# Moving the activation transposes of a fused matmul and rotary embedding from TensorE to VectorE

## The chip, the cores and the metric

The kernel runs on one core of a Trainium2 chip. The metric is the device time of one execution in microseconds (us). The kernel before takes 167.79 us (median of three runs, 167.52 to 168.66). Engine names in the profile lines are PE (TensorE matmul), PEld (TensorE weight load), DVE (VectorE), ACT (ScalarE), POOL (GpSimd) and SP (SyncE). ACTq and SPq are the queues from which ScalarE and SyncE issue their work, DMA transfers included. The span is the time from the first to the last instruction of the profiled execution, and the granted clock is the share of full TensorE speed that the chip's throttle allowed.

## The reference, cut to what matters

```python
batch, seq, hidden, n_heads = (16, 512, 768, 12)      # all arrays float32
y = np.matmul(x, weight)                              # (16*512, 768) @ (768, 768)
y = y.reshape(batch, seq, n_heads, head_dim)          # head_dim 64
y1, y2 = y[..., :32], y[..., 32:]
out1 = y1 * cos1 - y2 * sin1                          # cos, sin: (512, 64)
out2 = y2 * cos2 + y1 * sin2
out = np.concatenate([out1, out2], axis=-1)
```

The 8192 rows of x make 64 tiles of 128 rows, four tiles to a batch. The kernel's matmuls take x with the input columns on partitions, so each tile has to be transposed.

## The kernel before

A tile goes through these stages: SyncE loads it (393 KB), ScalarE casts it to fp16, TensorE transposes it in six 128x128 blocks by a matmul with the identity, ScalarE copies the result out of PSUM (the memory that matmuls write to), TensorE does 12 matmuls, VectorE does three multiplications (tv, and qv in two halves), GpSimd adds tv and qv, and ScalarE issues the store. The multiplications of a tile are called its rope below.

```python
    def stage_load(i):
        xs = xpool.tile([P, H], FP32, tag="xs")
        nc.sync.dma_start(out=xs, in_=xf[ts(i, P), :])          # 128 rows of 3072 B
    ...
    def stage_tp(i, eng):
        xc = x16[i]
        pt = pt_pool.tile([P, NKT, P], mm_dt, tag="pst")
        for kt in range(NKT):
            nc.tensor.transpose(pt[:, kt, :], xc[:, ts(kt, P)], ident)
        xT = tpool.tile([P, NKT, P], mm_dt, tag="xT")
        _copy(eng, xT, pt[:, :, :])
    ...
    for i in range(NMB):
        if i + 4 < NMB:
            stage_load(i + 4)
        if i + 2 < NMB:
            stage_cast(i + 2, nc.scalar)
        if i + 1 < NMB:
            stage_tp(i + 1, nc.scalar)
        stage_mm_rope(i)
        if i >= 3:
            stage_out(i - 3)            # nc.scalar.dma_start(...)
```

## Time and profile before

| | before |
|---|---|
| median time | 167.79 us |
| span of the profiled execution | 166.9 us |
| PE busy | 149.5 us (90%) |
| DVE busy | 125.4 us (75%) |
| one tile, start to start | 2.285 us |
| first tv starts at | 18.85 us |

These lines are from the page of the kernel before: the busy times of part 1, the chain of work that ended last (followed back from the last instruction, by engine), and five groups of instructions. A group's columns are line, engine, operation, tiles, shapes and count, then busy us and the mean ns of one, then the idle us just before them with what ended most of it.

```profile
PE 149.5 (90%) x1152; PEld 98.2 (59%) x1152; DVE 125.4 (75%) x202; ACT 97.2 (58%) x126; POOL 116.4 (70%) x68
...
PE 87%; DMA 4%; DVE 2%; ACT 1%; POOLq 1%; SPq 1%; issue 1%; DVEq 0%
...
L98 PE MATMUL psy<-w_sb,xT 128*128 128x512 f16 (+1 forms) x768 | 136.2, 328 | 0.0
...
L111 DVE TENSOR_TENSOR tv<-psy,cos_sb 128x768 f32<-128x768 f32 x64 | 61.2, 957 | 25.0 <-PE psy L98 23.2
L69 ACT COPY xT<-pt 128x768 f16<-128x768 f16 x63 | 50.2, 798 | 50.0 <-PE pt L87 41.7
L69 ACT CAST xc<-xs 128x768 f16<-128x768 f32 x62 | 51.7, 835 | 8.8 <-DMA xs<-in_x_dram 5.7
L87 PE MATMUL pt<-ident,xc 128*128 128x128 f16 x384 | 32.9, 224 | 10.2 <-DMA ident<-identity 9.1
```

TensorE is the engine that everything waits for: the chain is 87% PE, and VectorE's idle time is ended by psy, a matmul's result. The timeline of the kernel before shows one period. Its columns are start us, duration us, engine, line and operation, with idle time and releaser in brackets.

```profile
59.31 0.50 PE L87 MATMUL pt<-ident,xc 128*128 128x128 f16 x6
...
59.59 0.96 DVE L111 TENSOR_TENSOR tv<-psy,cos_sb 128x768 f32<-128x768 f32 x1 [0.40 <-PE psy L98]
...
59.65 2.11 PE L98 MATMUL psy<-w_sb,xT 128*128 128x512 f16 x12
...
61.60 0.50 PE L87 MATMUL pt<-ident,xc 128*128 128x128 f16 x6
...
61.87 0.96 DVE L111 TENSOR_TENSOR tv<-psy,cos_sb 128x768 f32<-128x768 f32 x1 [0.40 <-PE psy L98]
```

The six transposes start every 2.29 us, and the 12 matmuls start 0.34 us after them. VectorE is idle 0.40 us in each period.

### The profile page before, as it was taken

What the parts mean: (1) busy time and instruction counts of PE and PEld (TensorE: products, weight loads), DVE (VectorE), ACT (ScalarE), POOL (GpSimd) and SP (SyncE); (2) the same over time, 40 slices, a digit from 0 to 9 for tenths busy, and PEclk for the clock granted to TensorE, in tenths of its full rate; (3) what the DMA queues carried; (4) which work ended last, traced back from release to release, by engine and by line L of the source; (5) the groups of instructions that cost most, each with busy time, mean ns of one, the idle gap of its engine ahead of it and who ended that gap; (6) DMA issues with size and microseconds to landing.
All of it is one profiled execution on the core that took longest, in us unless ns stands there. A gap on an engine that the chain in (4) does not pass through costs nothing.

```text
span 166.9 us, 3238 instructions
## 1 busy us (share of the span) xinstructions
PE 149.5 (90%) x1152; PEld 98.2 (59%) x1152; DVE 125.4 (75%) x202; ACT 97.2 (58%) x126; POOL 116.4 (70%) x68
## 2 busy tenths in 40 slices
PE   0079799999999999999999999999999999999920
PEld 0065466666666666666666666666666666666610
DVE  1145499888898888888888888888888888888870
ACT  3150468666776666776666776666766667766100
POOL 0000099977778777787877788777787777887782
PEclk9999999999999999999999999999999999999997
DMA  5999789999999999999999999999999999834634
GB/s 190 300 394 404 290 286 262 381 379 368 335 356 376 321 343 351 339 350 337 348 342 351 373 331 339 361 325 348 350 329 376 320 352 320 341 152 164 244 151 170
DMA packets 20513, 53.20 MB, mean 319 GB/s; under 512 B 3345, under 2 KB 3345, under 8 KB 20497
## 3 DMA queue, kind: packets, MB, share of 16 engines
q1 hardware_dynamic: 11280, 27.82, 51.8%
q10 hardware_dynamic: 9216, 25.17, 37.7%
q8 instruction: 9, 0.15, 0.4%
q14 instruction: 8, 0.06, 0.1%
HBM read 27.82 MB, written 25.17 MB: 317 GB/s over the span
## 4 chain that ended last, share of the span: by engine, by line
PE 87%; DMA 4%; DVE 2%; ACT 1%; POOLq 1%; SPq 1%; issue 1%; DVEq 0%
PE psy L98 74%; PE pt L87 13%; DMA ident<-identity 4%; DVE tv L111 1%; POOLq L190 1%; ACT xc L69 1%; SPq L75 1%; DVE qv L116 1%; ACT xT L69 0%; DVEq L190 0%; DVE qv L113 0%; DVEq L111 0%
## 5 line engine op out<-in xcount | busy, mean ns | idle before, releaser
L120 POOL TENSOR_TENSOR ov<-tv,qv 128x768 f32<-128x768 f32 x64 | 116.2, 1817 | 47.0 <-DVE qv L116 45.0
L98 PE MATMUL psy<-w_sb,xT 128*128 128x512 f16 (+1 forms) x768 | 136.2, 328 | 0.0
L98 PEld LDWEIGHTS <-xT 128*128 128x128 f16 x768 | 73.1, 99 | 42.7 <-issue 1.3
L111 DVE TENSOR_TENSOR tv<-psy,cos_sb 128x768 f32<-128x768 f32 x64 | 61.2, 957 | 25.0 <-PE psy L98 23.2
L69 ACT COPY xT<-pt 128x768 f16<-128x768 f16 x63 | 50.2, 798 | 50.0 <-PE pt L87 41.7
L69 ACT CAST xc<-xs 128x768 f16<-128x768 f32 x62 | 51.7, 835 | 8.8 <-DMA xs<-in_x_dram 5.7
L87 PE MATMUL pt<-ident,xc 128*128 128x128 f16 x384 | 32.9, 224 | 10.2 <-DMA ident<-identity 9.1
L87 PEld LDWEIGHTS <-xc 128*128 128x128 f16 x384 | 27.6, 101 | 18.4 <-issue 5.1
L113 DVE TENSOR_TENSOR qv<-psy,tee_sb 128x384 f32<-128x384 f32 x64 | 35.0, 547 | 0.0
L116 DVE TENSOR_TENSOR qv<-psy,tee_sb 128x384 f32<-128x384 f32 x64 | 35.0, 547 | 0.0
L143 DVE CAST w_sb<-w_raw 128x768 f16<-128x768 f32 x6 | 3.4, 560 | 2.5 <-DMA w_raw<-in_weight_dram 2.5
L71 DVE CAST xc<-xs 128x768 f16<-128x768 f32 x2 | 1.1, 560 | 4.3 <-DMA xs<-in_x_dram 4.3
L71 DVE COPY xT<-pt 128x768 f16<-128x768 f16 x1 | 0.6, 558 | 4.5 <-PE pt L87 4.5
L69 ACT ACT_TABLE_LOAD x1 | 1.3, 1283 | 0.7 <-PEq L176 0.7
L176 POOL MEMSET const-float32-0.0<- 128x1 f32 x1 | 0.1, 98 | 0.2 <-issue 0.2
L144 DVE TENSOR_SCALAR tee_sb<-tee_sb 128x128 f32<-128x128 f32 x1 | 0.2, 218 | 0.0
L176 POOL MEMSET const-bfloat16-1.0<- 128x1 bf16 x1 | 0.1, 101 | 0.0
L176 POOL MEMSET const-uint8-127<- 128x1 uint8 x1 | 0.1, 101 | 0.0
L176 POOL MEMSET const-float32-1.0<- 128x1 f32 x1 | 0.1, 98 | 0.0
## 6 DMA issues: line engine op xcount, KB each, us to landing
xs<-in_x_dram SPq DMA_DIRECT2D x64, 384.0 KB, 5.3
out_dram<-ov ACTq DMA_DIRECT2D x64, 384.0 KB, 4.8
w_raw<-in_weight_dram SPq DMA_DIRECT2D x6, 384.0 KB, 6.8
cos_sb<-in_cos_dram SPq DMA_DIRECT2D x1, 128.0 KB, 6.4
tee_sb<-in_sin_dram SPq DMA_DIRECT2D x1, 128.0 KB, 6.4
ident<-identity SPq DMA_DIRECT2D x1, 32.0 KB, 6.4
```

Of the source, the lines that this page charges most:

```text
L69: eng.copy(out=o, in_=i_)
L71: eng.tensor_copy(out=o, in_=i_)
L75: nc.sync.dma_start(out=xs, in_=xf[ts(i, P), :])
L87: nc.tensor.transpose(pt[:, kt, :], xc[:, ts(kt, P)], ident)
L98: nc.tensor.matmul(psy[:, ds(noff, nsz)], xT[:, kt, :], w_sb[:, kt, ds(noff, nsz)], start=(kt == 0), stop=(kt == NKT - 1),)
L111: nc.vector.tensor_tensor(out=tv, in0=yh, in1=cbc, op=mybir.AluOpType.mult)
L113: nc.vector.tensor_tensor(out=qv[:, :, 0:HD], in0=yh[:, :, HD:D], in1=t1, op=mybir.AluOpType.mult)
L116: nc.vector.tensor_tensor(out=qv[:, :, HD:D], in0=yh[:, :, 0:HD], in1=t2, op=mybir.AluOpType.mult)
L120: nc.gpsimd.tensor_tensor(out=ov, in0=tv, in1=qv, op=mybir.AluOpType.add)
L143: nc.vector.tensor_copy(out=w_sb[:, kt], in_=w_raw[:, kt])
L176: nc = _bacc.Bacc("TRN2", target_bir_lowering=False, num_devices=1)
L190: with _tile.TileContext(nc) as tc:
```

## The change: intent and diff

The intent is to take all transposes off TensorE. The kernel uses the VectorE transpose as one within blocks of 32x32 elements, and leaves the rest of the transposition to the load: the 768 input columns of a batch are split into four quarters of 192, and quarter q is loaded onto partitions 32q to 32q+31. Two adjacent fp16 values are moved as one 4-byte element, so one instruction of 128x384 elements transposes a tile. The weights are loaded in a matching order. The work is now issued by batches of four tiles.

```diff
     def load(b, j0=0, nj=NJ):
...
+        for q in range(NQ):                       # four quarters, 32 partitions each
+            nc.sync.dma_start(
+                out=xss[b][ts(q, R), j0 : j0 + nj, :],
+                in_=x[b, ds(j0 * R, nj * R), ts(q, KQ)].rearrange("(j r) k -> r j k", r=R),
+            )
...
     def prepare(b, g0=0, ng=SB, eng=None):
...
+                nc.scalar.copy(out=x16[b][:, g], in_=src)
-            nc.tensor.transpose(pt[:, kt, :], xc[:, ts(kt, P)], ident)
+        nc.vector.transpose(
+            out=xTT[b][:, ds(g0, ng)].bitcast(FP32).rearrange("p g t j r -> p (g t j r)"),
+            in_=x16[b][:, ds(g0, ng)].bitcast(FP32).rearrange("p g t j r -> p (g t j r)"),
+        )
...
+    for i in range(NT, NMB - 1):
+        b, g = divmod(i, SB)
+        if g == 2 and 0 < b < B - 2:
+            load(b + 2)
+        ready = i + 1 if i == NT else i + 2
+        for n in range(ready, i + 3):
+            if n < NMB:
+                prepare(*divmod(n, SB), 1)        # cast and transpose of tile i + 2
+        for t in range(NT):
+            mm(i, t)
+        rope_whole(i)                             # tv and qv on VectorE, add on GpSimd
+        store(i - 3)                              # nc.scalar.dma_start(...)
```

The lines of this diff are picked from two whole kernels, with comments added, and cuts are marked with "...". The change also merges the two halves of qv into one VectorE instruction, moves the loads of the weights and of the cosine and sine tables to ScalarE's queue, sets other buffer counts, and computes the last tile in two halves.

More of the change, by code (lines that the diff above doesn't have):

```diff
@@ L7 @@
 import concourse.tile as tile
-from concourse import bass_utils, mybir
+from concourse import mybir
 from concourse.bass import ds, ts
@@ L13 @@
 FP16 = mybir.dt.float16
+MULT = mybir.AluOpType.mult
+ADD = mybir.AluOpType.add
 @with_exitstack
@@ L23 @@
     sin: bass.AP,
-    n_heads: bass.AP,
+    n_heads: int,
     out: bass.AP,
@@ L33 @@
     HD = D // 2
-    M = B * S
-    assert H % P == 0
-    NKT = H // P
-    NMB = M // P
+    R = 32
+    NQ = P // R
+    KQ = H // NQ
+    NT = KQ // (2 * R)
+    NMB = B * S // P
     SB = S // P
-    mm_dt = FP16
-    NSPLIT = [(0, 512), (512, H - 512)] if H > 512 else [(0, H)]
-    xf = x.rearrange("b s h -> (b s) h")
+    NSPLIT = [(0, 512), (512, H - 512)]
+    HALVES = [(0, H // 2), (H // 2, H // 2)]
     of = out.rearrange("b s h -> (b s) h")
     konst = ctx.enter_context(tc.tile_pool(name="konst", bufs=1))
-    ident = konst.tile([P, P], mm_dt)
@@ L50 @@
     cos_sb = konst.tile([P, SB, D], FP32)
     tee_sb = konst.tile([P, SB, D], FP32)
-    w_raw = konst.tile([P, NKT, H], FP32)
-    w_sb = konst.tile([P, NKT, H], mm_dt)
-    xpool = ctx.enter_context(tc.tile_pool(name="xpool", bufs=6))
-    cpool = ctx.enter_context(tc.tile_pool(name="cpool", bufs=3))
-    tpool = ctx.enter_context(tc.tile_pool(name="tpool", bufs=3))
-    opool = ctx.enter_context(tc.tile_pool(name="opool", bufs=4))
-    pt_pool = ctx.enter_context(tc.tile_pool(name="pt", bufs=2, space=bass.MemoryType.PSUM))
@@ L60 @@
-    py_pool = ctx.enter_context(tc.tile_pool(name="py", bufs=3, space=bass.MemoryType.PSUM))
-    xss = [None] * (NMB + 8)
-    x16 = [None] * (NMB + 8)
-    xTT = [None] * (NMB + 8)
-    ovs = [None] * NMB
-    def _copy(eng, o, i_):
-        if eng is nc.scalar:
-            eng.copy(out=o, in_=i_)
-        else:
-            eng.tensor_copy(out=o, in_=i_)
-    def stage_load(i):
-        xs = xpool.tile([P, H], FP32, tag="xs")
-        nc.sync.dma_start(out=xs, in_=xf[ts(i, P), :])
-        xss[i] = xs
@@ L78, in stage_cast @@
-    def stage_cast(i, eng):
-        xc = cpool.tile([P, H], mm_dt, tag="xc")
-        _copy(eng, xc, xss[i])
-        x16[i] = xc
-    def stage_tp(i, eng):
-        xc = x16[i]
-        pt = pt_pool.tile([P, NKT, P], mm_dt, tag="pst")
-        for kt in range(NKT):
-            nc.tensor.transpose(pt[:, kt, :], xc[:, ts(kt, P)], ident)
-        xT = tpool.tile([P, NKT, P], mm_dt, tag="xT")
-        _copy(eng, xT, pt[:, :, :])
-        xTT[i] = xT
-    def stage_mm_rope(i):
-        sb = i % SB
-        xT = xTT[i]
-        psy = py_pool.tile([P, H], FP32, tag="psy")
-        for kt in range(NKT):
-            for noff, nsz in NSPLIT:
-                nc.tensor.matmul(
-                    psy[:, ds(noff, nsz)],
-                    xT[:, kt, :],
-                    w_sb[:, kt, ds(noff, nsz)],
-                    start=(kt == 0),
-                    stop=(kt == NKT - 1),
-                )
-        yh = psy.rearrange("p (h d) -> p h d", d=D)
-        cbc = cos_sb[:, sb, :].unsqueeze(1).broadcast_to((P, NH, D))
-        t1 = tee_sb[:, sb, 0:HD].unsqueeze(1).broadcast_to((P, NH, HD))
-        t2 = tee_sb[:, sb, HD:D].unsqueeze(1).broadcast_to((P, NH, HD))
-        tv = tpool.tile([P, NH, D], FP32, tag="tv")
-        nc.vector.tensor_tensor(out=tv, in0=yh, in1=cbc, op=mybir.AluOpType.mult)
-        qv = tpool.tile([P, NH, D], FP32, tag="qv")
@@ new lines @@
+    w_raw = konst.tile([P, NT, 2, H], FP32)
+    w_sb = konst.tile([P, NT, 2, H], FP16)
+    xpool = ctx.enter_context(tc.tile_pool(name="xpool", bufs=3))
+    cpool = ctx.enter_context(tc.tile_pool(name="cpool", bufs=2))
+    tpool = ctx.enter_context(tc.tile_pool(name="tpool", bufs=2))
+    rpool = ctx.enter_context(tc.tile_pool(name="rpool", bufs=4))
+    opool = ctx.enter_context(tc.tile_pool(name="opool", bufs=5))
+    py_pool = ctx.enter_context(tc.tile_pool(name="py", bufs=4, space=bass.MemoryType.PSUM))
@@ new lines, with load, load_w @@
+    NJ = S // R
+    xss, x16, xTT, psys, ovs = {}, {}, {}, {}, {}
+    def load(b, j0=0, nj=NJ):
+        if b not in xss:
+            xss[b] = xpool.tile([P, NJ, KQ], FP32, tag="xs", name="xs")
+        for q in range(NQ):
[3 more added lines that the diff above has]
+            )
+    def load_w(t):
+        for q in range(NQ):
+            nc.scalar.dma_start(
+                out=w_raw[ts(q, R), t],
+                in_=weight[ds(q * KQ + t * 2 * R, 2 * R), :].rearrange(
+                    "(r e) n -> r e n", e=2
+                ),
+            )
@@ new lines, in prepare @@
+    def prepare(b, g0=0, ng=SB, eng=None):
+        if b not in x16:
+            x16[b] = cpool.tile([P, SB, NT, NQ, 2 * R], FP16, tag="xc", name="xc")
+            xTT[b] = tpool.tile([P, SB, NT, NQ, 2 * R], FP16, tag="xT", name="xT")
+        for g in range(g0, g0 + ng):
+            src = xss[b][:, ts(g, NQ), :].rearrange("p j (t r) -> p t j r", t=NT)
+            if eng is nc.vector:
+                nc.vector.tensor_copy(out=x16[b][:, g], in_=src)
+            else:
+                nc.scalar.copy(out=x16[b][:, g], in_=src)
+        nc.vector.transpose(
+            out=xTT[b][:, ds(g0, ng)].bitcast(FP32).rearrange("p g t j r -> p (g t j r)"),
+            in_=x16[b][:, ds(g0, ng)].bitcast(FP32).rearrange("p g t j r -> p (g t j r)"),
+        )
@@ new lines, in mm @@
+    def mm(i, t, parts=NSPLIT):
+        b, g = divmod(i, SB)
+        if i not in psys:
+            psys[i] = py_pool.tile([P, 2, 512], FP32, tag="psy", name="psy").rearrange(
+                "p b n -> p (b n)"
+            )
+        xT = xTT[b].rearrange("p g t j (r e) -> p g t j r e", e=2)
+        for e in range(2):
+            for noff, nsz in parts:
+                nc.tensor.matmul(
+                    psys[i][:, ds(noff, nsz)],
+                    xT[:, g, t, :, :, e].rearrange("p j r -> p (j r)"),
+                    w_sb[:, t, e, ds(noff, nsz)],
+                    start=(t == 0 and e == 0),
+                    stop=(t == NT - 1 and e == 1),
+                )
@@ L113, in stage_mm_rope, with rope @@
+    def rope(i, c0, n, ps, add_eng):
+        sb = i % SB
+        nh = n // D
+        tv = rpool.tile([P, H], FP32, tag="tv", name="tv")[:, :n]
+        qv = rpool.tile([P, H], FP32, tag="qv", name="qv")[:, :n]
         nc.vector.tensor_tensor(
-            out=qv[:, :, 0:HD], in0=yh[:, :, HD:D], in1=t1, op=mybir.AluOpType.mult
+            out=tv.rearrange("p (h d) -> p h d", d=D),
+            in0=ps.rearrange("p (h d) -> p h d", d=D),
+            in1=cos_sb[:, sb, :].unsqueeze(1).broadcast_to((P, nh, D)),
+            op=MULT,
@@ L115, in stage_mm_rope @@
         )
         nc.vector.tensor_tensor(
-            out=qv[:, :, HD:D], in0=yh[:, :, 0:HD], in1=t2, op=mybir.AluOpType.mult
-        )
-        ov = opool.tile([P, NH, D], FP32, tag="ov")
-        nc.gpsimd.tensor_tensor(out=ov, in0=tv, in1=qv, op=mybir.AluOpType.add)
-        ovs[i] = ov
-    def stage_out(i):
-        nc.scalar.dma_start(
-            out=of[ts(i, P), :], in_=ovs[i].rearrange("p h d -> p (h d)")
-        )
-    for i in range(4):
-        stage_load(i)
-    id_dram = nc.inline_tensor(np.eye(P, dtype=np.float16), name="identity")
@@ L132 @@
-    nc.sync.dma_start(out=ident, in_=id_dram.ap())
-    nc.sync.dma_start(out=cos_sb, in_=cos.rearrange("(sb p) d -> p sb d", p=P))
-    nc.sync.dma_start(out=tee_sb, in_=sin.rearrange("(sb p) d -> p sb d", p=P))
-    wv = weight.rearrange("(kt p) n -> p kt n", p=P)
-    for kt in range(NKT):
-        nc.sync.dma_start(out=w_raw[:, kt], in_=wv[:, kt])
-    stage_cast(0, nc.vector)
-    stage_cast(1, nc.vector)
-    stage_tp(0, nc.vector)
-    for kt in range(NKT):
-        nc.vector.tensor_copy(out=w_sb[:, kt], in_=w_raw[:, kt])
+            out=qv.rearrange("p (h t d) -> p h t d", t=2, d=HD),
@@ new lines, in rope, with rope_whole, store @@
+            in0=ps.rearrange("p (h t d) -> p h t d", t=2, d=HD)[:, :, ::-1, :],
+            in1=tee_sb[:, sb, :].rearrange("p (t d) -> p t d", t=2)
+            .unsqueeze(1).broadcast_to((P, nh, 2, HD)),
+            op=MULT,
+        )
+        ov = ovs[i]
+        add_eng.tensor_tensor(out=ov[:, ds(c0, n)], in0=tv, in1=qv, op=ADD)
+    def rope_whole(i):
+        ovs[i] = opool.tile([P, H], FP32, tag="ov", name="ov")
+        rope(i, 0, H, psys.pop(i)[:, 0:H], nc.gpsimd)
+    def store(i):
+        nc.scalar.dma_start(out=of[ts(i, P), :], in_=ovs.pop(i))
@@ new lines @@
+    for g in range(SB):
+        load(0, g * NQ, NQ)
+        if g < NT:
+            load_w(g)
+    nc.scalar.dma_start(out=cos_sb, in_=cos.rearrange("(sb p) d -> p sb d", p=P))
+    nc.scalar.dma_start(out=tee_sb, in_=sin.rearrange("(sb p) d -> p sb d", p=P))
+    load(1)
+    load(2)
+    for g in range(NT):
+        prepare(0, g, 1, nc.scalar)
+        for e in range(2):
+            nc.vector.tensor_copy(out=w_sb[:, g, e], in_=w_raw[:, g, e])
+        for t in range(g):
+            mm(g, t)
+        for i in range(g + 1):
+            mm(i, g)
@@ L146 @@
     )
-    for i in range(NMB):
-        if i + 4 < NMB:
-            stage_load(i + 4)
-        if i + 2 < NMB:
-            stage_cast(i + 2, nc.scalar)
-        if i + 1 < NMB:
-            stage_tp(i + 1, nc.scalar)
-        stage_mm_rope(i)
-        if i >= 3:
-            stage_out(i - 3)
-    for i in range(NMB - 3, NMB):
-        stage_out(i)
+    prepare(0, NT, 1, nc.scalar)
+    for i in range(NT):
+        rope_whole(i)
+    for i in range(NT, NMB - 1):
+        b, g = divmod(i, SB)
+        if g == 2 and 0 < b < B - 2:
[6 more added lines that the diff above has]
+            mm(i, t)
+        rope_whole(i)
+        store(i - 3)
+    i = NMB - 1
+    ovs[i] = opool.tile([P, H], FP32, tag="ov", name="ov")
+    ps = py_pool.tile([P, 2, 512], FP32, tag="psy", name="psy")
+    b, g = divmod(i, SB)
+    xT = xTT[b].rearrange("p g t j (r e) -> p g t j r e", e=2)
+    for n, (c0, sz) in enumerate(HALVES):
+        for t in range(NT):
+            for e in range(2):
+                nc.tensor.matmul(
+                    ps[:, n, 0:sz],
+                    xT[:, g, t, :, :, e].rearrange("p j r -> p (j r)"),
+                    w_sb[:, t, e, ds(c0, sz)],
+                    start=(t == 0 and e == 0),
+                    stop=(t == NT - 1 and e == 1),
+                )
+    for j in range(NMB - 4, NMB - 1):
+        store(j)
+    for n, (c0, sz) in enumerate(HALVES):
+        rope(i, c0, sz, ps[:, n, 0:sz], nc.vector)
+        nc.sync.dma_start(out=of[ts(i, P), ds(c0, sz)], in_=ovs[i][:, ds(c0, sz)])
 _INS = ['x', 'weight', 'cos', 'sin', 'n_heads']
```

## The prediction

> **What bounds the kernel now.** TensorE. The groups of instructions show PE busy 149.5 of 166.9 us; the chain of waits gives PE 87%. In the timeline one 128-row tile repeats every 2.285 us: 12 matmuls hold PE for 1.95 us, six identity transposes for most of the rest. VectorE sits idle 0.40 us per tile, waiting for PE. Its instructions overlap: tv (957 ns long) to the next start is 0.87 us, each 384-wide qv 0.46 us. The first tv starts at 18.85 us, the last PE work ends near 159.7 us.
>
> **Removed.** 384 transposes on PE (about 0.33 us per tile), the 0.80 us PSUM copy on ScalarE, the wait for the identity load (the chain's 6.4 us), one VectorE instruction per tile (two 384-wide qv become one 768-wide, 0.92 to 0.87 us start to start).
>
> **Added.** 64 VectorE transposes of 128x384 4-byte elements. None is in the trace. [...]
>
> **New bound.** PE falls to 1.95 us per tile. VectorE needs 0.87 + 0.87 + 0.50 = 2.24 us: nearly the old period, so almost all of the PE saving is eaten, and VectorE becomes the engine that sets the pace. 64 ropes (111 us) and 61 transposes (30 us) are 141 us after the first rope. Tail (half-tile work, last add, store) about 4 us.
>
> **Loads.** They worry me most. x now comes as 768 B runs, each transfer covering 32 partitions. The packet records of the trace show 256 B in 18 ns and 3072 B in 121 ns per DMA engine; a straight line gives 37 ns for 768 B. Then a tile needs 512 x 37 / 16 = 1.17 us of loading (was 0.97) plus 0.97 us of storing: 2.15 us of every 2.24. [...] The start (3.9 MB of x and weights, also in quarters) suffers likewise: I expect the first rope at 14 to 19 us.
>
> **Sum.** 16 + 141 + 4 us, about 2 us of small waits, 1 us between span and time: 164; the DMA risk moves the middle to 166. DMA-free best case 158; DMA-bound 175 to 182.
>
> **What would show it.** Right: VectorE busy over 85% with idle below 0.1 us per tile, tile period 2.2 to 2.35 us, PE at 12 matmuls per 1.95 us with gaps waiting for VectorE or for psy, transposes near 580 ns, the chain mostly VectorE. DMA-bound instead: ScalarE's cast idle waiting for x loads by tens of us, x landing times growing far above 5.3 us, DMA share pinned at 9 with GB/s below 340, period 2.4 us or more.
>
> **What would make it wrong.** [...] overlap lost around a transpose (+5 us); weight loads with a 4-byte step no longer hiding under matmuls (99 ns now); the 32-partition loads proving harmless (then 160) or fully serial (then over 180).

The sum came to 16 (first rope) + 141 (VectorE) + 4 (tail) + 2 (small waits) + 1 (span to time), or 164 us, and 166 with the DMA risk. A transpose of 580 ns, 0.50 us start to start (30 of the 141 us): estimates. Measured since are 574 ns (mean, kernel after) and 0.48 us (e1). The load rate behind the step to 166 and the range of 175 to 182 was not shown. Loads alone have since moved 208 to 221 GB/s in slices two to five of the kernel after.

## The result, and the profile after

| | before | after |
|---|---|---|
| median time | 167.69 us (4 runs of the same rounds) | 286.80 us (286.14 to 287.73, 4 runs) |
| ratio after / before | | 1.709 (95% interval 1.701 to 1.716) |
| span profiled | 166.9 us | 284.4 us |
| PE busy | 90% | 57% |
| DVE busy | 75% | 55% |
| first tv starts at | 18.85 us | 37.69 us |

A ratio is the mean time of one kernel's fast runs over the mean of the other's fast runs of the same rounds, so it is not quite the ratio of the medians quoted beside it. A run is marked slow when it is over 1.5% above the fastest of the same kernel. The result is correct, and the change costs 119 us.

These lines are from the page of the kernel after. They answer to the ones shown of before. The digits after PEclk are the granted TensorE clock in tenths, in 40 slices of 7.1 us, and GB/s has one number per slice.

```profile
PE 161.5 (57%) x768; PEld 85.2 (30%) x768; DVE 156.8 (55%) x203; ACT 49.8 (18%) x65; POOL 114.0 (40%) x67
...
PEclk9999999959796987959796886959797795968898
...
GB/s 165 218 221 220 208 19 169 333 224 218 350 217 253 218 219 171 220 153 231 125 221 211 202 240 144 244 133 227 142 217 225 180 250 17 118 103 55 168 26 195
...
L107 PE MATMUL psy<-w_sb,xT 128*128 128x512 f16 x756 | 159.5, 383 | 116.4 <-DVE xT L93 116.4
...
L120 DVE TENSOR_TENSOR tv<-psy,cos_sb 128x768 f32<-128x768 f32 (+1 forms) x65 | 61.2, 942 | 44.0 <-PE psy L107 39.9
L92 ACT CAST xc<-xs 128x768 f16<-128x768 f32 x64 | 48.5, 828 | 199.7 <-DMA out_dram<-ov 181.8
L93 DVE STREAM_TRANSPOSE xT<-xc 128x384 f32<-128x384 f32 x64 | 36.5, 574 | 54.2 <-ACT xc L92 54.2
```

No engine is near its limit: PE, the busiest, is busy for 57% of the span. Every idle time points one stage upstream: PE waits for the transposes, the transposes wait for the casts, and the casts on ScalarE were idle 181.8 us until a store had been issued. A cast does not need a store's data. It only stands behind the store in ScalarE's queue, and it starts once the store is issued, not landed: 0.19 us after the issue in the round below, where the quickest store of the run took 1.9 us to land. The timeline of the kernel after shows one whole round of a batch.

```profile
97.23 6.48 ACTq L141 DMA_DIRECT2D out_dram<-ov  x4
...
103.91 3.03 ACT L92 CAST xc<-xs 128x768 f16<-128x768 f32 x4 [13.08 <-DMA out_dram<-ov]
104.77 0.58 DVE L93 STREAM_TRANSPOSE xT<-xc 128x384 f32<-128x384 f32 x1 [3.36 <-ACT xc L92]
...
105.41 10.66 PE L107 MATMUL psy<-w_sb,xT 128*128 128x512 f16 x48 [5.92 <-DVE xT L93]
...
109.54 0.96 DVE L120 TENSOR_TENSOR tv<-psy,cos_sb 128x768 f32<-128x768 f32 x1 [1.99 <-PE psy L107]
...
113.34 6.96 ACTq L141 DMA_DIRECT2D out_dram<-ov  x4
...
114.23 5.70 POOL L134 TENSOR_TENSOR ov<-tv,qv 128x768 f32<-128x768 f32 x3 [0.92 <-DVE qv L126]
...
116.17 0.96 DVE L120 TENSOR_TENSOR tv<-psy,cos_sb 128x768 f32<-128x768 f32 x1
...
120.49 0.83 ACT L92 CAST xc<-xs 128x768 f16<-128x768 f32 x1 [13.55 <-DMA out_dram<-ov]
```

Follow the batch that is cast at 103.91. Its matmuls start at 105.41, its four ropes run from 109.54 on, and GpSimd's fourth add ends at 119.93 (114.23 + 5.70). The last of its four stores is issued by 120.30, and only then, at 120.49, does the next batch's first cast run. One batch takes 16.58 us from cast to cast, or 4.1 us per tile, and apart from the loads no stage of one batch overlaps a stage of the next. From the third batch's first cast (55.95 us) to the end (284.4 us) the 14 batches take 16.3 us each.

The built order of ScalarE's queue shows the same thing before any run. In the listing of the kernel after, "TensorCopy" is the cast and "DMACopy" the store:

```
L92 TensorCopy xc<-xs 128x768 x8
L141 DMACopy out_dram<-ov 128x768 x8
L92 TensorCopy xc<-xs 128x768 x4
L141 DMACopy out_dram<-ov 128x768 x4
L92 TensorCopy xc<-xs 128x768 x4
...
```

The listing is the build's own and not a view of a trace, but ScalarE's timeline of the run after shows the same order:

```profile
29.17 3.03 ACT L92 CAST xc<-xs 128x768 f16<-128x768 f32 x4 [4.19 <-DMA xs<-in_x_dram]
41.43 14.40 ACTq L141 DMA_DIRECT2D out_dram<-ov  x8
55.95 3.03 ACT L92 CAST xc<-xs 128x768 f16<-128x768 f32 x4 [23.75 <-DMA out_dram<-ov]
```

ScalarE took its work as listed: in the trace, groups of four casts and four stores alternate to the last cast (267.08 us). The source alternates cast(i + 2) and store(i - 3). The build grouped them by batch. Casts 12 to 15 stand behind stores 8 to 11, and the last of those needs the last add of its own batch.

There is a second, smaller loss inside each round. TensorE had been idle 5.92 us before 105.41. Split into windows, the granted clock of the kernel after is 0.50 from 105.4 to 109.5 us and 1.00 from 112 to 116 us, so the first tile of the batch needed 4.13 us of matmuls. A window's line gives the stretch, its length, the busy time and count of PE, PEld, DVE, ACT and POOL, then the granted clock, the DMA share and GB/s.

```profile
105.40:109.50 4.10, 4.09 (x13) 1.96 (x14) 1.73 (x3) 1.54 (x3) 0.00 (x0) 0.50 0.27 81
...
112.00:116.00 4.00, 4.00 (x26) 2.25 (x23) 3.60 (x4) 0.00 (x0) 3.08 (x2) 1.00 1.10 222
```

The trace sets this beside the idle time before: after the gap of 5.92 us the clock is 0.50, and so it is from 57.4 to 61.4 us, after a gap of 5.97 us, while the second batch's 48 matmuls (at 43.51 us), after a gap of only 2.61 us, took 7.97 us in all. No run shows where between the two gaps the change lies.

The 48 matmuls of the 13 whole rounds from 57.45 us on take 9.26 to 10.89 us, 10.3 on average, and the rounds follow: the round with 9.26 lasts 15.2 us, the one with 10.89 lasts 16.8. By an estimate from these numbers, 2.3 us a round (10.3 less the 7.97 of the second batch) or some 30 us in all are the half clock. It is part of what the order costs: the mean granted clock is 0.851 here and 0.849 in e3, whose casts stand behind the stores in the same way, against 0.985 to 0.990 in e1, e2 and e4, whose casts run ahead of those stores.

### The profile page after: what moved, and what is told of

Read it like the earlier page. It is cut to its first block, busy times and chain, and to the rows that moved or that the text cites. A ratio compares the mean times of both kernels' runs of the same rounds, so it can differ in the third digit from the quotient of the medians.

```text
span 284.4 us, 2299 instructions
## 1 busy us (share of the span) xinstructions
PE 161.5 (57%) x768; PEld 85.2 (30%) x768; DVE 156.8 (55%) x203; ACT 49.8 (18%) x65; POOL 114.0 (40%) x67
## 5 line engine op out<-in xcount | busy, mean ns | idle before, releaser
L107 PE MATMUL psy<-w_sb,xT 128*128 128x512 f16 x756 | 159.5, 383 | 116.4 <-DVE xT L93 116.4
L134 POOL TENSOR_TENSOR ov<-tv,qv 128x768 f32<-128x768 f32 x63 | 113.8, 1809 | 165.6 <-DVE qv L126 161.4
L107 PEld LDWEIGHTS <-xT 128*128 128x128 f16 x756 | 84.0, 113 | 191.5 <-DVE xT L93 122.5
L120 DVE TENSOR_TENSOR tv<-psy,cos_sb 128x768 f32<-128x768 f32 (+1 forms) x65 | 61.2, 942 | 44.0 <-PE psy L107 39.9
L92 ACT CAST xc<-xs 128x768 f16<-128x768 f32 x64 | 48.5, 828 | 199.7 <-DMA out_dram<-ov 181.8
L93 DVE STREAM_TRANSPOSE xT<-xc 128x384 f32<-128x384 f32 x64 | 36.5, 574 | 54.2 <-ACT xc L92 54.2
L126 DVE TENSOR_TENSOR qv<-psy,tee_sb 128x768 f32<-128x768 f32 (+1 forms) x65 | 60.7, 934 | 0.0
L187 PE MATMUL psy<-w_sb,xT 128*128 128x384 f16 x12 | 2.1, 326 | 0.0
L187 PEld LDWEIGHTS <-xT 128*128 128x128 f16 x12 | 1.2, 98 | 0.8
L134 DVE TENSOR_TENSOR ov<-tv,qv 128x384 f32<-128x384 f32 x2 | 1.4, 690 | 0.0
```

Of the source, the lines that this page charges most:

```text
L92: nc.scalar.copy(out=x16[b][:, g], in_=src)
L93: nc.vector.transpose(out=xTT[b][:, ds(g0, ng)].bitcast(FP32).rearrange("p g t j r -> p (g t j r)"), in_=x16[b][:, ds(g0, ng)].bitcast(FP3 ...
L107: nc.tensor.matmul(psys[i][:, ds(noff, nsz)], xT[:, g, t, :, :, e].rearrange("p j r -> p (j r)"), w_sb[:, t, e, ds(noff, nsz)], start=(t = ...
L120: nc.vector.tensor_tensor(out=tv.rearrange("p (h d) -> p h d", d=D), in0=ps.rearrange("p (h d) -> p h d", d=D), in1=cos_sb[:, sb, :].unsqu ...
L126: nc.vector.tensor_tensor(out=qv.rearrange("p (h t d) -> p h t d", t=2, d=HD), in0=ps.rearrange("p (h t d) -> p h t d", t=2, d=HD)[:, :, : ...
L134: add_eng.tensor_tensor(out=ov[:, ds(c0, n)], in0=tv, in1=qv, op=ADD)
```

## The experiments

Two theories were tested. The first is the order theory: the built order of ScalarE's queue serializes the batches. The rival is the load theory: x loaded in four transfers of 32 partitions, in packets of 768 B (61 ns, median, in the kernel after), is too slow. The second had been the main worry of the prediction, and the page of the kernel after gives it some support, since loads alone moved only 208 to 221 GB/s in slices two to five.

Four experiments load x in another arrangement than the weights and give a wrong result (e2, e3, e4, e11). They are for time only. All others are correct.

### e1: the same kernel in source order

```diff
-                nc.scalar.copy(out=x16[b][:, g], in_=src)
+                tc.keep_in_program_order(nc.scalar.copy(out=x16[b][:, g], in_=src))
...
-        nc.vector.transpose(
+        tc.keep_in_program_order(nc.vector.transpose(
...            (the same around tv's tensor_tensor and around the store's dma_start)
```

This keeps ScalarE's casts and stores, and VectorE's transposes and tv, in the order of the source. No instruction, size, buffer or transfer changes. Two queues are pinned at once here; e3 and e5 below change only the queues of casts and stores.

> The changed kernel with one thing altered: the ScalarE casts and stores and the VectorE transposes and first products are kept in the order in which the source states them (cast of tile i+2, store of tile i-3, and so on). Loads unchanged. Theory A (order): the loss comes from the built order, in which the four casts of a batch queue on ScalarE behind the four stores of the batch before, so that batches do not overlap at all (16 us per batch of 4 tiles). Then this run takes 175 to 210 us: first rope still near 33 us, afterwards 2.3 us per tile if VectorE sets the pace, up to 2.9 us if loads (768 B at 60 ns a packet) do. Theory B (loads): the 32-partition loads hold the casts up; then the order matters little and it stays above 260 us.

Measured: 184.41 us in the profiled run, which is the only one marked fast. The three timed rounds took 187.96, 188.09 and 190.22 us and were marked slow because they are over 1.5% above it (clock 0.973 to 0.983 against 0.988). The ratio, 1.126 (1.119 to 1.134), is of those three. The fast run is 1.100 times the 167.62 us of before. Either way the order alone is worth about 100 us of the 119. In the kernel after TensorE has a gap of 5.9 to 6.3 us before every batch from the third on. In e1, with every buffer count unchanged, it is busy 58.30 of the 60 us from 60 to 120. The timeline of e1 shows the queue taking casts and stores in turn, and VectorE working without a gap:

```profile
47.44 0.34 ACTq L141 DMA_DIRECT2D out_dram<-ov  x1
47.82 0.83 ACT L92 CAST xc<-xs 128x768 f16<-128x768 f32 x1 [1.58 <-POOL ov L134]
49.63 0.34 ACTq L141 DMA_DIRECT2D out_dram<-ov  x1
50.02 0.83 ACT L92 CAST xc<-xs 128x768 f16<-128x768 f32 x1 [1.37 <-POOL ov L134]
...
100.61 0.92 DVE L120 TENSOR_TENSOR tv<-psy,cos_sb 128x768 f32<-128x768 f32 x1
101.45 0.94 DVE L126 TENSOR_TENSOR qv<-psy,tee_sb 128x768 f32<-128x768 f32 x1
102.32 0.56 DVE L93 STREAM_TRANSPOSE xT<-xc 128x384 f32<-128x384 f32 x1
102.80 0.92 DVE L120 TENSOR_TENSOR tv<-psy,cos_sb 128x768 f32<-128x768 f32 x1
```

The period is 2.19 us (100.61 to 102.80): 0.84 for tv, 0.87 for qv and 0.48 for the transpose, start to start. That is the regime the prediction described. The casts still wait behind stores, but at this stage each wait is shorter than a period, so nothing is lost. What remains of the loss looks like the start: the first tv begins at 37.58 us, 18.7 us later than before. But the chain of e1 is mostly x's loads, by line:

```profile
DMA xs<-in_x_dram 74%; DMA tee_sb<-in_sin_dram 5%; PE psy L107 4%; DVE qv L126 3%; SPq L69 2%; POOL ov L134 2%; DVE tv L120 2%; DVE xT L93 1%; DVE ov L134 1%; ACT xc L92 1%; ACTq L141 0%; DVEq L134 0%; DVE tee_sb L160 0%; ACTq L92 0%
```

So the loads are barely ahead of VectorE here, and e6 and e7 will show that an earlier start alone gains little.

### e2, e3, e4: fast loads, with three orders

```diff
-        for q in range(NQ):
+        for g in range(j0 // NQ, (j0 + nj) // NQ):
             nc.sync.dma_start(
-                out=xss[b][ts(q, R), j0 : j0 + nj, :],
-                in_=x[b, ds(j0 * R, nj * R), ts(q, KQ)].rearrange("(j r) k -> r j k", r=R),
+                out=xss[b][:, ts(g, NQ), :].rearrange("p j k -> p (j k)"),
+                in_=x[b, ts(g, P), :],
             )
```

e2 loads x as before does: 128 partitions, 3072 B rows. Its order is left to the build. e3 adds an order-only dependency that puts the casts of each batch behind the last store of the batch before it. e4 is e2 with the source order of e1.

> The changed kernel with x loaded by 128-partition transfers of 3072 B rows (wrong result on purpose, same bytes). The order is left to the scheduling pass, which now puts the casts up to two batches ahead of the stores. Theory A and theory B both expect 160 to 180 us, with packets back at 121 ns; this run alone tells nothing, it is the partner of the next one.

> As the run before (fast 128-partition loads, wrong result on purpose), but the casts of each batch are made to queue behind the last store of the batch before, as they were built in the changed kernel. Theory A: about 15 to 16 us per batch again, 250 to 275 us in all, PE clock below 0.9. Theory B: no longer slow, below 190 us.

> Source order kept as in the first run and fast 128-partition x loads (wrong result on purpose). Both theories: 158 to 175 us; VectorE busy above 85% after the start, tile period 2.2 to 2.35 us. The difference from the first run is what the quarter loads cost once the order is right: 10 to 35 us.

Measured: e2 178.43 us (1.065, 1.060 to 1.069), e3 280.32 us (1.673, 1.662 to 1.683), e4 180.89 us (1.079, 1.074 to 1.084). e3 and e4 each came 5 to 6 us above the expected range; in e4 the first tv is still at 36.1 us.

e2 alone would have misled. The loads changed and the time fell by 108 us, which reads like a proof of the load theory. But the build also chose another order: in e2's listing, and in its timeline, the queue starts with 15 casts and then mixes single casts with runs of stores, so casts stay batches ahead of the stores. e3 keeps the fast loads and puts the bad order back, and the time goes up again by 102 us. The list of waits of e3 (engine and line, what it waited for, us in total, times, longest) begins with the same wait as the kernel after (its line numbers are one higher), and its timeline shows the rounds again:

```profile
ACT xc L93 <- DMA out_dram<-ov: 191.0, 14, 21.0
...
110.92 6.18 ACTq L142 DMA_DIRECT2D out_dram<-ov  x4
117.19 3.03 ACT L93 CAST xc<-xs 128x768 f16<-128x768 f32 x4 [12.20 <-DMA out_dram<-ov]
```

So under the bad order the loads are worth only about 6.5 us (286.80 less 280.32), and under the source order 3.5 us (184.41 in e1's fast run less 180.89 in e4), where 10 to 35 had been expected. The second figure rests on one fast run of e1. Why the scheduling pass groups the casts with quarter loads and not with full-width ones was not tested. Only the two built orders were seen.

### e5: one word, the stores on another queue

```diff
     def store(i):
-        nc.scalar.dma_start(out=of[ts(i, P), :], in_=ovs.pop(i))
+        nc.sync.dma_start(out=of[ts(i, P), :], in_=ovs.pop(i))
```

> The changed kernel with one word altered: the stores are issued from SyncE's queue, not ScalarE's. No order is pinned. Built, ScalarE now holds nothing but casts after its start, VectorE still takes the transposes in groups of four, SyncE interleaves four loads with four stores. Theory A (the casts wait on ScalarE behind stores that wait for the last add of the batch before): 185 to 215 us, PE clock back above 0.95. Rival A2 (any grouping by batches serializes, whichever engine holds the stores): stays above 240 us.

Measured: 208.94 us (1.246, 1.236 to 1.257). Nothing was pinned, yet most of the loss is gone, because casts no longer share a queue with stores. A smaller form of the same fault takes its place: x loads are now in SyncE's queue with the stores. There the stores wait 77.3 us in 47 waits for GpSimd's adds, and the list of waits of e5 says that the casts wait for the loads.

```profile
ACT xc L92 <- DMA xs<-in_x_dram: 87.7, 11, 15.0
```

This supports the order theory from another side: what matters is which work stands behind which wait in the same queue.

### e6, e7: an earlier start

e6 is e1 with the weights loaded by three transfers of 128 partitions, not twelve of 32. To allow this, partition p takes weight rows 6p to 6p+5, and the cast picks its columns in the matching order.

```diff
     def load_w(t):
-        for q in range(NQ):
-            nc.scalar.dma_start(
-                out=w_raw[ts(q, R), t],
...
+        nc.scalar.dma_start(
+            out=w_raw[:, t],
+            in_=weight.rearrange("(p s) n -> p s n", s=2 * NT)[:, ts(t, 2)],
+        )
...
-            src = xss[b][:, ts(g, NQ), :].rearrange("p j (t r) -> p t j r", t=NT)
+            src = xss[b].rearrange("p j k -> p (j k)")[:, ts(g, H)].rearrange(
+                "p (r t e) -> p t r e", t=NT, e=2
+            )
...            (and the cast's output view in the matching order)
```

e7 is e6 with VectorE's start in source order: weight casts and transposes first, then the sign change of the sine table, which waits for a late load and had stood ahead of the transposes.

```diff
...            (the weight casts are pinned in the same way)
-    nc.vector.tensor_scalar_mul(
-        out=tee_sb[:, :, 0:HD], in0=tee_sb[:, :, 0:HD], scalar1=-1.0
-    )
     prepare(0, NT, 1, nc.scalar)
+    tc.keep_in_program_order(
+        nc.vector.tensor_scalar_mul(
+            out=tee_sb[:, :, 0:HD], in0=tee_sb[:, :, 0:HD], scalar1=-1.0
+        )
+    )
```

> e1_pinned plus weights loaded by 128-partition transfers: the input columns are dealt to partitions as 6 neighbours each, so the weight rows of a partition are neighbours too (correct result, cast reads another stride). Theory C (what is left of the loss is the start: 3.9 MB arriving in quarters): weight packets move at 40 ns per 1024 B again (6144 B in 446 ns before), first rope from 37.6 us to 28 to 33 us, total 178 to 184 us. If the start is not what is left: 186 to 190 us as before.

> e6_pinned_w plus the start of VectorE in source order: the transpose of the first tile stands ahead of the six weight casts and of the sign flip of the sine table (which waited 4.3 us for that table in e1_pinned). Theory C: PE starts earlier, first rope at 24 to 29 us, total 172 to 180 us. If the order at the start costs nothing beyond the loads: as e6_pinned_w.

Measured: e6 181.33 us (1.082, 1.071 to 1.092), e7 183.73 us (1.096, 1.088 to 1.104). e6's first tv starts at 20.63 us, so the weights' transfers alone bring the start forward by 17 us and gain 3 us of total time. The reordered start of e7 gains nothing on top: its first tv starts at 22.71 us. e7 is a miss that teaches: with a start 15 us earlier than in e1, it ends with e1's time. The timeline of e7 shows VectorE at its period of 2.19 us and then a hole (41.99 to 46.99):

```profile
39.80 0.92 DVE L120 TENSOR_TENSOR tv<-psy,cos_sb 128x768 f32<-128x768 f32 x1
...
41.99 0.92 DVE L120 TENSOR_TENSOR tv<-psy,cos_sb 128x768 f32<-128x768 f32 x1
...
46.99 0.92 DVE L120 TENSOR_TENSOR tv<-psy,cos_sb 128x768 f32<-128x768 f32 x1
```

The list of waits of e7 begins with the casts waiting for x:

```profile
ACT xc L91 <- DMA xs<-in_x_dram: 64.1, 13, 7.7
```

Its chain by line begins with x's loads too:

```profile
DMA xs<-in_x_dram 85%; DMA tee_sb<-in_sin_dram 3%; DVE qv L126 3%; SPq L69 1%; DVE tv L120 1%; DVE ov L134 1%; DVE xT L93 1%; ACT xc L91 1%; DVEq L134 0%; ACTq L91 0%
```

In e1 the late start gave the loads a lead that the rest of the run lived on: its casts waited 29.4 us for x, against 64.1 in e7. In e7 the start no longer hides the load rate, and the 15 us are given back in waits for x. Here the load theory is right, as the second limit, once the first is gone. No run repeats e7 with 128-partition loads of x and nothing else changed, so how much of this limit is the 32-partition span stays open.

### e8, e9, e10: loads from two queues, and the start again

e8 is e7 with two of x's four quarters issued from SyncE and two from ScalarE, the weights split over both queues, and the loads of batches 1 and 2 moved behind the casts of batch 0.

```diff
         for q in range(NQ):
-            nc.sync.dma_start(
+            (nc.sync if q < 2 else nc.scalar).dma_start(
                 out=xss[b][ts(q, R), j0 : j0 + nj, :],
```

e9 is e8 with batch 0 loaded in four whole quarters, ahead of three weight transfers on alternating queues. e10 is e9 with all weights on ScalarE's queue and the tables on SyncE's. This is e10's start against that of the kernel after:

```diff
-    for g in range(SB):
-        load(0, g * NQ, NQ)
-        if g < NT:
-            load_w(g)
-    nc.scalar.dma_start(out=cos_sb, ...)
-    nc.scalar.dma_start(out=tee_sb, ...)
-    load(1)
-    load(2)
+    load(0)
+    for t in range(NT):
+        load_w(t)
+    nc.sync.dma_start(out=cos_sb, ...)
+    nc.sync.dma_start(out=tee_sb, ...)
...                                    (casts and transposes of batch 0)
+    load(1)
+    load(2)
```

> e7_pinned_w_start plus two issue queues for x and weights: two quarters of x from SyncE, two from ScalarE, so that both halves of the partitions are written at the same time; the loads of batches 1 and 2 issued after the first batch's casts. Theory D[...]: 768 B packets fall from about 60 ns to 37 to 45 ns, first rope at 16 to 20 us, period 2.19 us, total 158 to 167 us, below the kernel before. Rival[...]: packets stay near 60 ns, first rope at 22 us or later, total 168 us or more.

Theory D expects that quarters of x loaded from two queues land faster, the rival that they do not.

> e8_two_queues with another start: batch 0 of x as four whole-quarter loads (two per queue) instead of sixteen small ones, then the weights in three 128-partition loads, then the tables, so that ScalarE's casts wait behind 5 issues, not 14. Theory C (what e8 still loses is its start: first rope at 29.1 us): first rope at 16 to 20 us, period 2.19 us as in e8, total 160 to 168 us, level with or a little below the kernel before. If the start is bound by the bytes (4 MB of 256 to 768 B pieces at 200 to 250 GB/s) rather than by the issue chain: first rope stays at 22 us or later and the total at 169 us or more.

> e9_fast_start with the start's transfers dealt out again: all weights on ScalarE's queue behind its two quarters of x, the two tables on SyncE's queue behind its own two. In e9 ScalarE's quarters of batch 0 landed only at 13.5 us because SyncE's queue, done with its half, was already moving weights in 6144 B packets between ScalarE's 768 B packets. Theory C2 (that sharing delays the first cast): first cast from 14.8 us to about 9 us, first rope from 23.2 us to 16 to 19 us, total 162 to 166 us, below the kernel before. If not: first rope stays at 22 us or later, total 168 to 170 us.

Measured: e8 175.9 us (the median of four runs, of which two were fast, 173.53 and 175.0; ratio of the fast ones 1.040, 1.030 to 1.049), e9 169.14 us (1.009, 1.004 to 1.014), e10 168.41 us against 167.65 of before (1.005, 1.000 to 1.010, five rounds). All three missed the time that their theory gave; the first tv came at 29.1 us in e8 and 23.2 us in e9, where 16 to 20 had been expected. In e9 ScalarE waits for x until 13.52 us and the first cast starts at 14.82; in e10 it starts at 9.41, as theory C2 expected, though the first tv is late. In e8 the casts' wait for x fell to 13.8 us, from 64.1 in e7, but e8 changed the weights' queues and the start as well, and its profiled run was slow, so what the two queues are worth by themselves was not shown.

e8's profiled run was slow, so its span is not compared. Its packet records, and those of e1, e7 and e11, from 60 to 140 us of each run give the time of a 768 B packet (10th, 50th and 90th percentile, and mean):

```
kernel                        768 B packets, ns: p10 / p50 / p90, mean     GB/s moved
e1  one queue, late start     36 / 36 / 64   43                            342
e7  one queue, early start    36 / 36 / 71   49                            319
e8  two queues                36 / 36 / 47   40 (SyncE)                    354
                              36 / 38 / 58   43 (ScalarE)
e11 128-partition transfers   36 / 36 / 36   39                            352
```

The GB/s here are not the most that the loads could do: VectorE's period of 2.19 us asks for 393 KB in and 393 KB out per tile, or 359 GB/s. Only e7 stays well below.

e10 starts level with before: its first tv is at 19.18 us. The period then should give 0.1 us per tile (2.285 less 2.188), some 6 us by this arithmetic over 60 tiles. The timeline of e10 shows where most of that goes:

```profile
22.64 0.95 DVE L120 TENSOR_TENSOR tv<-psy,cos_sb 128x768 f32<-128x768 f32 x1
...
26.30 0.58 DVE L93 STREAM_TRANSPOSE xT<-xc 128x384 f32<-128x384 f32 x1 [1.84 <-ACT xc L91]
...
27.58 0.92 DVE L120 TENSOR_TENSOR tv<-psy,cos_sb 128x768 f32<-128x768 f32 x1
...
30.84 0.96 DVE L120 TENSOR_TENSOR tv<-psy,cos_sb 128x768 f32<-128x768 f32 x1 [1.00 <-PE psy L107]
```

Batch 1's x arrives late, and the two steps from 22.64 to 30.84 take 8.20 us, where two periods are 4.38: 3.8 us are lost. The rest lies in the kernel before, whose first five steps are quicker than its period: 8.98 us from the first tv (18.85) to the sixth (27.83), where five periods are 11.43. So e10's sixth tv, at 33.07 us, is 5.2 us behind, and the period wins that back by the end. From 40 to 120 us VectorE is busy every microsecond (80.00 of 80) and TensorE 77.93. No version beat before; e10 equals it.

### e11: small packets or few partitions?

e11 is e1 with x in the same 768 B pieces, but each transfer spans 128 partitions.

```diff
-                out=xss[b][ts(q, R), j0 : j0 + nj, :],
-                in_=x[b, ds(j0 * R, nj * R), ts(q, KQ)].rearrange("(j r) k -> r j k", r=R),
+                out=xss[b][:, ts(q, NQ), :],
+                in_=x[b].rearrange("(g p) k -> p g k", p=P)[:, :, ts(q, KQ)],
```

> e1_pinned with x loaded in the same 768 B pieces, but by transfers that span all 128 partitions (wrong result on purpose, same bytes and packets). Theory D[...]: 768 B packets at 36 to 40 ns from the start of the steady state on, total 176 to 184 us. Rival D2 (small packets are slow by themselves): packets stay at 50 to 60 ns and the total at 186 us or more.

Theory D is that the 32-partition span makes a packet take 60 ns.

Measured: 184.46 us (1.100, 1.092 to 1.108). In total time this does not differ from e1's fast run of 184.41 us, so as a test of time it is inconclusive. e1 and e11 both start late (first tv at 37.58 and 38.66 us) and then run at VectorE's pace. The packets do tell the cases apart: in the loads-only stretch from 25 to 40 us the median 768 B packet takes 62 ns in e1 and 42 ns in e11, and in the table above nine in ten of e11's packets need no more than 36 ns. The packet's size is the same, so it is the 32-partition span of the transfers, not the small piece, that goes with packets of 60 ns. The weights say the same: their 6144 B packets took 433 ns (median) in e1, by transfers of 32 partitions, and 265 ns in e6, by transfers of 128.

## Why the prediction was wrong, point by point

The predicted middle was 166 us, with 158 as the best case and 175 to 182 if DMA set the pace. Measured were 286.8 us. That e10 ends near 166 us does not confirm the sum: it has another order, other load queues and another start.

- **What bounds the kernel before** was right: TensorE, at 2.285 us per tile.
- **The cost of the added instruction** was right: 580 ns predicted, 574 measured (mean), and 0.48 us start to start in e1 where 0.50 was predicted.
- **TensorE without transposes** was right. The 12 matmuls of a tile fit into the period (PE busy 58.30 of 60 us in e1, VectorE all 60), and weight loads with a 4-byte step stayed hidden (a tile's twelve take 1.74 us in e1's timeline, 1.78 in before's).
- **"VectorE needs 0.87 + 0.87 + 0.50 = 2.24 us"** was right as a limit. e1, e7 and e10 run at 2.19 us. The kernel after never reaches it.
- **"Sum. 16 + 141 + 4 us" is the step that failed.** It adds VectorE's work as if VectorE always had work, which takes for granted that cast, transpose, matmul, rope and store of different tiles overlap. That is a property of the order of the queues. The prediction does not mention the order that the build chose. In that order a batch's casts stand behind the stores of the batch before, so a round of four tiles takes 16.3 us where four periods of e1 take 8.75. Over 14 batches that is 106 us, of 119 lost. e1 (286.8 to 184.4 by order alone) and e3 against e2 (178.4 to 280.3 by order alone) show it. The overlap that the prediction listed as a risk was the one around a transpose (+5 us), not this one.
- **The "first rope at 14 to 19 us"** was a mis-sized term: 37.7 us measured. The weights and x, all in 32-partition transfers, came at about 220 GB/s, and the sign change of a table waited for its load ahead of the transposes. e6 changed the weights' part and the first tv moved from 37.58 to 20.63 us; e7 took the sign change out of the way as well, which brought no further gain (22.71). An earlier start is not a gain in total time by itself: e7 gave it back.
- **The loads** were the right worry at the wrong rank. The effect of 32-partition transfers exists (median packet of 62 ns in e1, 42 in e11), and in e7 waits for x's loads do set the total. In the kernel after the loads were worth 6.5 us.
- **What would show it** helped even so. The prediction named "ScalarE's cast idle waiting for x loads by tens of us" as the sign of the load theory. The cast was idle, by 199.7 us, but waiting for stores. The view was right, and the releaser named there pointed to the order theory before the experiments showed it.
- **The half clock** was not in the prediction. It adds about 2.3 us per round by the estimate above, some 30 of the 106 us, but goes with the gaps that the order makes: in e1 the mean granted clock is 0.988, against 0.851 in the kernel after.

## What to carry to other kernels

Before adding up what each engine must do, list the built order of every engine's queue and ask of each instruction what it stands behind: here stores that waited for the end of a tile held the casts behind them for 181.8 us, and issue order in the source says little where a scheduler may group it. When a change of data layout also changes the built order, test the order separately (here by pinning it, and by putting the bad order on the fast layout), or the layout gets the blame. And when a first wait is removed, expect the gain to run into the next limit (here the loads, and then the start) before it reaches the total.
